# One ring of seven latent buffers instead of four and three, and five small cached loads issued by gpsimd instead of sync

## The chip, the cores and the metric

The kernel runs on 1 core of one Trainium2 chip. The metric is the device time of one execution in microseconds, shown as the median of the runs of the kernel before. The profile is of one further execution.

## The reference, cut to what matters

Two layers of a streaming encoder are computed for one prompt of 512 frames and one sample of 64 frames (576 columns in all; 128 further positions come from caches). Layer A is chunk-band attention; layer B, in which the change lies, is latent attention:

```python
def b_project(h, pos, w_in, g_qa, w_uq, g_kva, g_qn, g_qr, g_kr):
    cq, ckv, kr, g = jnp.split(h @ w_in, [B_Q_RANK, B_Q_RANK + B_KV_RANK, B_Q_RANK + B_KV_RANK + B_ROPE], axis=-1)
    q = (rmsnorm(cq, g_qa) @ w_uq).reshape(b, s, B_HEADS, B_QK)
    q_nope = rmsnorm(q[..., :B_NOPE], g_qn)
    q_rope = rope(rmsnorm(q[..., B_NOPE:], g_qr), pos)
    ckv = rmsnorm(ckv, g_kva)
    k_rope = rope(rmsnorm(kr, g_kr), pos)
    return q_nope, q_rope, ckv, k_rope, g

# sample: ckv and k_rope are put behind the cached latents
ckv_all = jnp.concatenate([ckv_cache.astype(ckv.dtype), ckv], axis=1)
kr_all = jnp.concatenate([kr_cache.astype(k_rope.dtype), k_rope], axis=1)
# every layer: y = x + (silu(g) * attention(...)) @ w_out
```

The ranks of cq and ckv are 512 each, there are 16 heads, the no-position part of a head has 128 elements and the rotary part 64.

## The kernel before, in words

All tensors are held transposed: 128 partitions of features by 576 columns of tokens. Every float32 product is made as three matmuls of a high and a low part (`mm3`, line 226, through `matmul`, line 164), so each operand is first split: ACT makes the high part (line 203, or 208 with a gain) and DVE the low part (lines 204, 209). A weight block of 128 x 512 is loaded by sync (`wload`, line 217) into one of three raw buffers and split into one of five pairs.

The work of TensorE is put in order by hand: the class `Order` (line 42) holds streams (Python generators) with ranks and a clock of its own, and the stream of the lowest rank that is due emits its next matmuls. The orders of the other engines and of the two DMA queues (sync and gpsimd) come from a scheduler that sees the tile pools. A tile of a pool with n buffers waits until the last reader of the buffer that it gets is done. Engines and queues run strictly in order: one waiting instruction holds all behind it.

Layer B begins at line 860, when layer A's sum lies in DRAM as x1d. Its 16 parts are loaded again on the gpsimd queue (line 885, tiles `bx`, one `raw` buffer each) and split into `bh` and `bl` with the gain of the norm. Three kinds of streams then run side by side:

- `latents` (line 976) multiplies 11 blocks of `wb_in` with all 16 parts (tiles `lat`, 96 matmuls each): 0 to 3 give cq, then 8 the rotary key, 4 to 7 ckv, and 9 and 10 the first two gates. In the stage of the queries it fills the time between their blocks.
- `queries` (line 985) follows when cq is normed: 24 blocks (tiles `u`, 24 matmuls each) in eight rounds of one rotary pair `r` and two heads `q`.
- every block has a chain. `raw_of` (line 490) is ACT's copy out of PSUM into a `raw` buffer, which gives the PSUM buffer back; there are two of them (tag `mm`), and an unfinished `lat` block holds one, so a `u` block needs the copy of the `u` before it. Then ACT squares and splits (lines 457, 203), DVE makes the low part (204), TensorE sums over the partitions (tiles `st`), ACT does Ln, Exp, Square (470, 478, 480) and DVE two steps and the scaling (481, 484, 488). `query_chain` (line 1002) writes the raw buffer to DRAM on the gpsimd queue (line 1007, tensor `qd`). `rotary_chain` (line 1011) swaps 32-row pieces by four DMAs of the sync queue (`sw`, line 916), combines them on DVE (917 to 919), splits the result (`hi` on ACT, `lo` on DVE) and writes four pieces on the sync queue (`qrd`, lines 1023, 1024). `rotary_key` (line 957) does the same with the key and writes `krT` on gpsimd (line 963).

The `raw` buffers lie in two pools, one of four and one of three (`lr0`, `lr1`, line 870). The 16 `bx` take turns by the list `turn`; cqraw and ckvraw name the four (`of=0`), krraw and every q and r the three (`of=1`). A ckvraw keeps its buffer until all four are scaled, after the last query.

The cached latents `cc` (four of 128 x 128, line 946) and the cached rotary key `krc` (line 966) share one buffer of their own and are loaded by the sync queue.

Of the kernel before, what the change touches and what calls it, by code (L numbers as in the profile page):

```python
# [15 lines left out]
F32 = mybir.dt.float32  # L16
# [4 lines left out]
P = 128  # L21
# [4 lines left out]
N = NS + NP  # L26
# [92 lines left out]
def encoder(tc, xT, wa_in, wa_out, wb_in, wuq, wuk, wuqr, wuv, wb_out, kcT, vc, ckvcT, krcT, gains, rtab,  # L119
            ident, cosT, sinT, yT, kT, vT, ckvT, krT):  # L120
    nc = tc.nc
# [4 lines left out]
    def pool(name, bufs=1, side="left", space=None):  # L126
        kw = dict(name=name, bufs=bufs)
        if space is None:
            kw["side"] = side
            kw["reuse_waits"] = "tile"  # L130
        else:
            kw["space"] = space
        g = tc.tile_pool(**kw)
        return g, g.__enter__()

    def close(g):
        g.__exit__(None, None, None)
# [17 lines left out]
    def two(ap):  # L155
        return ap.rearrange("p (c n) -> p c n", c=2)
# [44 lines left out]
    def split(src, hi, lo):  # L201

        ACT.copy(hi, src)  # L203
        V.tensor_tensor(out=lo, in0=src, in1=hi.bitcast(F32), op=ALU.subtract)  # L204
# [209 lines left out]
    def square_sum(acc, src, tp, w, first, name):  # L414

        if first:
            ACT.activation(acc, src, AF.Square)
            return
        sq = tp("s1", F32, name + "sq")[:, :w]
        ACT.activation(sq, src, AF.Square)  # L420
        V.tensor_tensor(out=acc, in0=acc, in1=sq, op=ALU.add)

    def col_sums(sq, tp, w, ones_ap, name, wait=2.0):

        s2 = tp("s2", F32R, name + "s2")[:, :w]
        s3 = tp("s3", F32R, name + "s3")[:, :w]
        split(sq, s2, s3)
        h = w // 2
        yield od_.now + wait
        yield "st"  # L430
        st = ps_of("st", name + "st")
        for j, s in enumerate((s2, s3)):
            for c in range(2):
                matmul(st[:, c, :h], ones_ap, s[:, c * h:(c + 1) * h], start=j == 0, stop=j == 1)
        return st, sq, s2
# [19 lines left out]
    def squares(src, tp, w, ones_ap, name):  # L455
        sq = tp("s1", F32, name + "sq")[:, :w]
        ACT.activation(sq, src, AF.Square)
        return (yield from col_sums(sq, tp, w, ones_ap, name, L_SQ))

    def rnorm(sums, n, w, base=None, coef=None, keep=None):  # L460

        st, t, y = sums
        h = w // 2
        plain = base is None and keep is None
        ms = st[:, :, :h]
        if plain:
            ACT.activation(two(t), ms, AF.Ln, scale=1.0 / n, bias=epst[:, 0:1])  # L470
        else:
            if base is None:
                V.tensor_scalar_add(two(keep), ms, n * EPS)
                ms = two(keep)
            else:
                V.scalar_tensor_tensor(out=ms, in0=two(base), scalar=coef, in1=ms, op0=ALU.mult, op1=ALU.add)
            ACT.activation(two(t), ms, AF.Ln, scale=1.0 / n)
        ACT.activation(y, t, AF.Exp, scale=-0.5)
        y = y.bitcast(F32)
        ACT.activation(t, y, AF.Square)  # L480
        V.scalar_tensor_tensor(out=two(t), in0=ms, scalar=n * EPS if plain else 0.0, in1=two(t),
                               op0=ALU.add, op1=ALU.mult)
        od_.give("st", L_ST)
        V.scalar_tensor_tensor(out=t, in0=t, scalar=3.0 * n, in1=y, op0=ALU.subtract, op1=ALU.mult)
        return t

    def scaled(raw, col, z):
        V.scalar_tensor_tensor(out=raw, in0=raw, scalar=col, in1=z, op0=ALU.mult, op1=ALU.mult)

    def raw_of(ps, tp, w, name, **kw):  # L490
        raw = tp("raw", F32, name, **kw)[:, :w]
        ACT.copy(two(raw), ps[:, :, :w // 2])  # L492
        od_.give("mm", L_M)
        return raw
# [372 lines left out]
    close(g_T)  # L867
    g_x1, x1p = pool("x1", side="right")
    g_l, lp = pool("lat")
    g_r0, lr0 = pool("latraw0")  # L870
    g_r1, lr1 = pool("latraw1")
    turn = [1, 1, 1, 0, 0, 0, 0]

    def tpl(tag, dt, name, of=None):
        if tag == "raw":
            turn.append(turn.pop(0))
            k = turn[-1] if of is None else of
            return (lr0, lr1)[k].tile([P, N], dt, tag=tag, bufs=(4, 3)[k], name=name)
        bufs = {"s1": SB, "s2": SB, "s3": S3}.get(tag, 1)
        return lp.tile([P, N], dt, tag=tag, bufs=bufs, name=name)  # L880

    h = []
    for m in range(KT):
        x1 = tpl("raw", F32, f"bx{m}")
        nc.gpsimd.dma_start(x1, x1d[m * P:(m + 1) * P, :])
        hi = x1p.tile([P, N], F32R, tag="x1", bufs=32, name=f"bh{m}")
        lo = x1p.tile([P, N], F32R, tag="x1", bufs=32, name=f"bl{m}")
        split_g(x1, gn[:, G_LNB + m:G_LNB + m + 1], hi, lo)
        h.append((hi, lo))
# [21 lines left out]
    def rope(x, name):  # L911

        sw = tpl("sw", F32, name + "sw")
        for j in range(4):
            i = j ^ 1
            nc.sync.dma_start(sw[j * 32:(j + 1) * 32, :], x[i * 32:(i + 1) * 32, :])
        V.tensor_tensor(out=x, in0=x, in1=cos, op=ALU.mult)
        V.tensor_tensor(out=sw, in0=sw, in1=sin, op=ALU.mult)
        V.tensor_tensor(out=x, in0=x, in1=sw, op=ALU.add)
# [2 lines left out]
    ckv_acc = lp.tile([P, N], F32, name="ckv_acc")  # L922

    def q_latent(m, ps):
        raw = raw_of(ps, tpl, N, f"cqraw{m}", of=0)
        raws.append(raw)
        square_sum(cq_acc, raw, tpl, N, m == 0, f"cq{m}")
        if m < 3:
            return
        mine = raws[:]  # L930
        raws.clear()
        yield lambda: flag["ln"]
        st = yield from col_sums(cq_acc, tpl, N, ones, "cq", 6.0)
        z = rnorm(st, 512, N, base=EX, coef=512 * EPS / D)
        for j in range(4):
            scaled(mine[j], gcq[:, j:j + 1], z)
            split(mine[j], *cq[j])
        yield od_.now + L_CQ
        flag["cq"] = True

    def kv_latent(m, ps):
        raw = raw_of(ps, tpl, N, f"ckvraw{m}", of=0)
        raws.append(raw)
        square_sum(ckv_acc, raw, tpl, N, m == 0, f"ckv{m}")
        cc = lp.tile([P, NC], F32, tag="cc", bufs=1, name=f"cc{m}")
        nc.sync.dma_start(cc, ckvcT[m * P:(m + 1) * P, :])
        split(cc, ckv[m][0][:, :NC], ckv[m][1][:, :NC])
        if m < 3:
            return
        st = yield from col_sums(ckv_acc, tpl, N, ones, "ckv", 6.0)  # L950
        z = rnorm(st, 512, N, base=EX, coef=512 * EPS / D)
        for j in range(4):
            scaled(raws[j], gkva[:, j:j + 1], z)
            nc.gpsimd.dma_start(ckvT[j * P:(j + 1) * P, :], raws[j])
            split(raws[j], ckv[j][0][:, NC:], ckv[j][1][:, NC:])

    def rotary_key(ps):

        raw = raw_of(ps, tpl, N, "krraw", of=1)
        st = yield from squares(raw, tpl, N, blk, "kr")  # L960
        scaled(raw, gkr, rnorm(st, 64, N, base=EX, coef=64 * EPS / D))
        rope(raw, "kr")
        nc.gpsimd.dma_start(krT, raw[:64, :])
        split(raw, KR[0][:, NC:], KR[1][:, NC:])
        cc = lp.tile([P, NC], F32, tag="cc", bufs=1, name="krc")
        nc.sync.dma_start(cc, krcT)
        split(cc, KR[0][:, :NC], KR[1][:, :NC])

    def gate_of(hd, ps, tp):
# [31 lines left out]

    def query_chain(hd, ps):
        n_ = f"q{hd}"
        raw = raw_of(ps, tpl, N, n_ + "raw", of=1)
        st = yield from squares(raw, tpl, N, ones, n_)
        scaled(raw, gqn, rnorm(st, P, N))
        nc.gpsimd.dma_start(qd[hd * P:(hd + 1) * P, :], raw)
        yield od_.now + L_CH
        flag["rot"] += 1

    def rotary_chain(pr, ps):
        n_ = f"r{pr}"
        raw = raw_of(ps, tpl, N, n_ + "raw", of=1)
        st = yield from squares(raw, tpl, N, blk, n_)
        scaled(raw, gqr, rnorm(st, 64, N))
        rope(raw, n_)
        hi = tpl("qrh", F32R, n_ + "hi")
        lo = tpl("qrl", F32R, n_ + "lo")
        split(raw, hi, lo)
        for j in range(2):  # L1020
            a = slice(j * 64, j * 64 + 64)
            r0 = (2 * pr + j) * P
            nc.sync.dma_start(qrd[r0:r0 + 64, :], hi[a, :].bitcast(F32))
            nc.sync.dma_start(qrd[r0 + 64:r0 + 128, :], lo[a, :].bitcast(F32))
        yield od_.now + L_CH
        flag["rot"] += 1
# [2 lines left out]
    od_.spawn(5, latents())  # L1029
    od_.spawn(3, queries())  # L1030
    od_.run()
    close(g_r1)
    close(g_r0)
    close(g_l)


# [226 lines left out]
DIRECT, GA, WRAW, WHL, SGB, DEEP, VA = 2, 2, 3, 5, 2, 2, 2  # L1263
LAT = (0, 1, 2, 3, 8, 4, 5, 6, 7, 9, 10)
LAHEAD = 1
SB, S1H, S2H, S3 = 4, 3, 1, 1
S1A, S2A, S3A, L_RS = 3, 2, 1, 5.0
L_SQ, L_RN, L_SP, L_X, L_SM, L_T, L_RE, L_CH, L_ST = 7.0, 11.5, 4.6, 2.3, 3.5, 2.9, 1.2, 4.0, 4.0

# [81 lines left out]
```

## Time and profile before

| what | value |
|---|---|
| three runs | 2080.25, 2077.2, 2077.83 us; median 2077.83 us |
| profiled execution | 2074.61 us, its span 2072.8 us, granted clock 0.987 |
| PE (TensorE) | 2002.1 us busy (97%), 14692 matmuls |
| DVE (VectorE) | 1353.6 us busy (65%), 2651 instructions |
| ACT (ScalarE) | 1107.8 us busy (53%), 2034 instructions |
| POOL (GpSimd) | 91.8 us busy (4%), 173 instructions |
| sync queue | 171.78 MB, 30.6% of the 16 DMA engines' time |
| gpsimd queue | 49.20 MB, 6.8% |

The span runs from the first to the last instruction; 1.8 us of the execution lie around it. Layer A takes the time up to about 1137 us, the latents and queries of layer B that from 1146 to 1426 us, the heads of layer B and its output the rest. A matmul of 288 columns follows the one before it every 0.13 us at the upper of the two clock levels (2.4 GHz) and every 0.27 us at the lower (1.2 GHz), so a busy PE can still lose time.

### The profile page before, as it was taken

How to read it: one execution, taken by the hardware profiler on the slowest of the kernel's cores; microseconds unless marked ns; L12 is line 12 of the kernel's file. 1: busy time of each engine (PE TensorE's matmuls, PEld its weight loads, DVE VectorE, ACT ScalarE, POOL GpSimd, SP SyncE). 2: the span in 40 equal slices, each digit the busy share in tenths (PEclk: the TensorE clock that was granted, in tenths of full speed). 3: DMA queues.
4: the chain of work that ended last, by engine and by line, in shares of the span. 5: the costliest groups of instructions: out<-in, count | busy, mean ns of one | idle time of the engine just before them, and what ended most of it. 6: DMA issues, size and time to landing. Idle time of an engine off the chain costs nothing. (4 is left out here: it accounts for less than half of the span.)

```text
span 2072.8 us, 37566 instructions
## 1 busy us (share of the span) xinstructions
PE 2002.1 (97%) x14692; PEld 1979.3 (95%) x14692; DVE 1353.6 (65%) x2651; ACT 1107.8 (53%) x2034; POOL 91.8 (4%) x173
## 2 busy tenths in 40 slices
PE   8999999999999999999999898889999999999998
PEld 8999999999999999999999898889999999998998
DVE  7665555555555555559777456667776767676875
ACT  6644454454544444456444457666666656664432
POOL 0000000000000000000001000000000000002000
PEclk9999999999999999999999999999999999999999
DMA  7333333333333333324553434444232332256541
GB/s 209 86 83 88 93 84 89 93 78 88 89 88 88 90 87 86 87 73 139 156 155 112 147 84 127 127 112 145 76 91 81 90 90 80 74 154 217 173 139 61
DMA packets 119345, 223.38 MB, mean 108 GB/s; under 512 B 14272, under 2 KB 29264, under 8 KB 119168
## 3 DMA queue, kind: packets, MB, share of 16 engines
q1 hardware_dynamic: 104752, 171.78, 30.6%
q0 software_dynamic: 14416, 49.20, 6.8%
q8 instruction: 115, 1.88, 0.4%
q14 instruction: 62, 0.51, 0.1%
HBM read 183.92 MB, written 34.36 MB: 105 GB/s over the span
## 5 line engine op out<-in xcount | busy, mean ns | idle before, releaser
L204 DVE TENSOR_TENSOR wa_2l<-wa_2r,wa_2h 128x512 fp32r<-128x512 f32 x61 | 42.2, 692 | 92.2 <-ACT wa_2h L203 92.2
L203 ACT CAST wa_2h<-wa_2r 128x512 fp32r<-128x512 f32 x61 | 37.7, 619 | 103.7 <-PE a2p L164 10.1
L204 DVE TENSOR_TENSOR wa_3l<-wa_3r,wa_3h 128x512 fp32r<-128x512 f32 x61 | 42.2, 692 | 43.8 <-ACT wa_3h L203 42.3
L203 ACT CAST wa_0h<-wa_0r 128x512 fp32r<-128x512 f32 x61 | 37.8, 619 | 61.3 <-PE a2p L164 4.3
L203 ACT CAST wa_3h<-wa_3r 128x512 fp32r<-128x512 f32 x61 | 37.7, 618 | 51.2 <-PE a2p L164 4.5
L164 PE MATMUL u<-cqh,wq_0h 128*128 128x288 f32 x128 | 31.7, 333 | 24.6 <-ACT r4raw L492 5.2
L204 DVE TENSOR_TENSOR wa_0l<-wa_0r,wa_0h 128x512 fp32r<-128x512 f32 x61 | 41.9, 687 | 18.0 <-ACT wa_0h L203 18.0
L203 ACT CAST wa_1h<-wa_1r 128x512 fp32r<-128x512 f32 x61 | 37.8, 620 | 25.0 <-PE a0pg L164 2.6
L204 DVE TENSOR_TENSOR wa_1l<-wa_1r,wa_1h 128x512 fp32r<-128x512 f32 x61 | 41.9, 686 | 11.7 <-ACT wa_1h L203 11.7
L164 PEld LDWEIGHTS u<-cqh,wq_0h 128*128 128x128 f32 x128 | 23.6, 217 | 26.4 <-ACT r4raw L492 5.4
L164 PE MATMUL u<-cql,wq_0h 128*128 128x288 f32 x128 | 30.5, 324 | 0.0
L164 PE MATMUL u<-cqh,wq_0l 128*128 128x288 f32 x128 | 30.3, 322 | 0.0
L204 DVE TENSOR_TENSOR wb_1l<-wb_1r,wb_1h 128x512 fp32r<-128x512 f32 x25 | 17.2, 688 | 19.9 <-ACT wb_1h L203 19.8
L204 DVE TENSOR_TENSOR wb_3l<-wb_3r,wb_3h 128x512 fp32r<-128x512 f32 x25 | 17.2, 687 | 17.6 <-ACT wb_3h L203 17.5
L164 PE MATMUL lat<-bh,wb_0h 128*128 128x288 f32 x88 | 19.5, 304 | 9.1 <-ACT bh L208 9.1
L203 ACT CAST wb_1h<-wb_1r 128x512 fp32r<-128x512 f32 x25 | 15.5, 619 | 23.4 <-PE lat L164 10.0
L203 ACT CAST wb_3h<-wb_3r 128x512 fp32r<-128x512 f32 x25 | 15.4, 617 | 23.3 <-PE lat L164 11.2
L204 DVE TENSOR_TENSOR wb_2l<-wb_2r,wb_2h 128x512 fp32r<-128x512 f32 x25 | 17.1, 686 | 13.0 <-ACT wb_2h L203 13.0
L164 PE MATMUL g<-bh,wb_1h 128*128 128x288 f32 x112 | 24.3, 298 | 0.0
L164 PE MATMUL g<-bh,wb_0h 128*128 128x288 f32 x112 | 24.3, 298 | 0.0
L164 PE MATMUL g<-bh,wb_2h 128*128 128x288 f32 x112 | 24.2, 298 | 0.0
L164 PE MATMUL g<-bh,wb_3h 128*128 128x288 f32 x112 | 24.2, 298 | 0.0
(6782 smaller groups left out, 8058.5 us busy)
## 6 DMA issues: line engine op xcount, KB each, us to landing
wa_0r<-wa_in SPq DMA_DIRECT2D x61, 256.0 KB, 2.9
wa_1r<-wa_in SPq DMA_DIRECT2D x61, 256.0 KB, 2.9
wa_2r<-wa_in SPq DMA_DIRECT2D x61, 256.0 KB, 2.9
wa_3r<-wa_in SPq DMA_DIRECT2D x61, 256.0 KB, 2.9
wb_0r<-wb_in SPq DMA_DIRECT2D x25, 256.0 KB, 3.0
wb_1r<-wb_in SPq DMA_DIRECT2D x25, 256.0 KB, 3.0
wb_2r<-wb_in SPq DMA_DIRECT2D x25, 256.0 KB, 2.9
wb_3r<-wb_in SPq DMA_DIRECT2D x25, 256.0 KB, 2.9
```

What stands on the lines that cost most here:

```text
L164: nc.tensor.matmul(out, lhs, rhs, start=start, stop=stop, **kw)
L203: ACT.copy(hi, src)
L204: V.tensor_tensor(out=lo, in0=src, in1=hi.bitcast(F32), op=ALU.subtract)
```

## The change

The two pools become one pool of seven buffers, and the list `turn` and the argument `of` go: each `raw` tile gets whichever of the seven the scheduler gives it. The five small loads `cc` and `krc` move from the sync queue to the gpsimd queue.

```diff
-    g_r0, lr0 = pool("latraw0")
-    g_r1, lr1 = pool("latraw1")
-    turn = [1, 1, 1, 0, 0, 0, 0]
-
-    def tpl(tag, dt, name, of=None):
+    g_r, lrp = pool("latraw")
+
+    def tpl(tag, dt, name):
         if tag == "raw":
-            turn.append(turn.pop(0))
-            k = turn[-1] if of is None else of
-            return (lr0, lr1)[k].tile([P, N], dt, tag=tag, bufs=(4, 3)[k], name=name)
+            return lrp.tile([P, N], dt, tag=tag, bufs=RAWB, name=name)
...
-        nc.sync.dma_start(cc, ckvcT[m * P:(m + 1) * P, :])
+        nc.gpsimd.dma_start(cc, ckvcT[m * P:(m + 1) * P, :])
...
-        raw = raw_of(ps, tpl, N, n_ + "raw", of=1)
+        raw = raw_of(ps, tpl, N, n_ + "raw")
...
-        nc.sync.dma_start(cc, krcT)
+        nc.gpsimd.dma_start(cc, krcT)
...
-SB, S1H, S2H, S3 = 4, 3, 1, 1
+RAWB, SB, S1H, S2H, S3 = 7, 4, 3, 1, 1
```

The order of TensorE's instructions is the same in both programs. On the other engines the scheduler gives another order. Three places follow.

The first is ACT in the stage of the queries, where the second rotary pair is copied out of PSUM (`r2raw<-u`); q3's and q2's rows are the norms of heads 3 and 2, `wb`, `wr` and `wq` are weight blocks.

```order
 L203 CAST wb_3h<-wb_3r 128x512
+L492 COPY r2raw<-u_14640 128x576
+L457 ACTIVATE r2sq<-r2raw 128x576
+L203 CAST r2s_14675<-r2sq 128x576
 L203 CAST wr_0h<-wr_0r 128x512
 L470 ACTIVATE q3sq<-q3st,epst 128x576
+L478 ACTIVATE q3s_14606<-q3sq 128x576
+L480 ACTIVATE q3sq<-q3s_14606 128x576
 L203 CAST r1hi<-r1raw 128x576
-L492 COPY r2raw<-u_14643 128x576
-L457 ACTIVATE r2sq<-r2raw 128x576
-L203 CAST r2s_14678<-r2sq 128x576
```

The copy and the two rows behind it stand ahead of the norm of q3 and of r1's split now, where they stood behind them; the copies of r3 to r7 move in the same way. In the program before, r2raw waits for the write of q2 to DRAM, two blocks back; in the changed one for that of q0, five blocks back.

The second is ACT at the start of layer B, before and (the second fence) in the change: `KRh` is the high part of the cached rotary key, `ckvh` that of a cached latent, and `lnb_s` the last row that belongs to layer A's sum.

```order
L203 CAST lnb_s_13309<-lnb_acc 128x576
L203 CAST KRh<-krc 128x128
L208 ACTIVATE bh_13329<-bx_13327,gn 128x576
L208 ACTIVATE bh_13335<-bx_13333,gn 128x576
L208 ACTIVATE bh_13341<-bx_13339,gn 128x576
L203 CAST ckvh_13299<-cc_14467 128x128
```

```order
L203 CAST lnb_s_13309<-lnb_acc 128x576
L208 ACTIVATE bh_13326<-bx_13324,gn 128x576
L208 ACTIVATE bh_13332<-bx_13330,gn 128x576
L203 CAST KRh<-krc 128x128
L208 ACTIVATE bh_13338<-bx_13336,gn 128x576
L208 ACTIVATE bh_13344<-bx_13342,gn 128x576
```

The first two `bh` stand ahead of `KRh` now, and the four `ckvh` have gone behind the last `bh`.

The third is the gpsimd queue at the same place in the changed program.

```order
L834 DMA x1d<-x_15_13046 128x576
L891 DMA sin<-sinT 128x576
L962 DMA krc<-krcT 128x128
L881 DMA bx_13366<-x1d 128x576
...
L881 DMA bx_13414<-x1d 128x576
L942 DMA cc_14464<-ckvcT 128x128
```

`krc` is new between `sin` and the eighth `bx`, and the four `cc` follow the last `bx`; the next row of that queue, `krT`, comes some 80 us later in the profile of before.

## Rows read from the trace of the kernel before

**Rows 1.** Busy time by stretch: PE, PEld, DVE, ACT, POOL, then PEclk, DMA share, GB/s.

```profile
1233.00:1410.40 177.40, 147.07 (x1013) 144.71 (x1012) 120.67 (x172) 123.53 (x196) 8.72 (x16) 0.91 0.46 124
1165.00:1228.00 63.00, 63.00 (x475) 63.00 (x475) 25.43 (x37) 24.59 (x42) 0.00 (x0) 1.00 0.32 81
...
1390.00:1400.00 10.00, 10.00 (x77) 10.00 (x77) 5.75 (x8) 8.44 (x14) 0.00 (x0) 1.00 0.30 73
```

**Rows 2.** Waits of PE over the span: us in total, times, longest us.

```profile
PE lat L164 <- ACT bh L208: 9.1, 1, 9.1
...
PE u L164 <- ACT q1raw L492: 5.6, 1, 5.6
...
PE u L164 <- ACT r6raw L492: 4.8, 1, 4.8
...
PE u L164 <- ACT r5raw L492: 3.4, 1, 3.4
...
PE u L164 <- ACT q6raw L492: 0.2, 1, 0.2
```

**Rows 3.** Chain of waits, 1312 to 1339 us: start, us, what.

```profile
1312.08 4.06 DMA qd<-q6raw
...
1316.91 5.07 PE u L164 x24
1321.98 2.40 PE lat L164 x18
1324.38 0.54 PE r4st L164 x4
1324.92 3.19 PE u L164 x24
1328.11 1.60 PE lat L164 x12
```

**Rows 4.** Timeline of ACT around two of the waits: start, us, instruction, [idle before].

```profile
1309.38 0.62 ACT L203 CAST wq_0h<-wq_0r 128x512 fp32r<-128x512 f32 x1 [0.74 <-PE u L164]
...
1316.22 0.64 ACT L492 COPY r4raw<-u 128x576 f32<-128x576 f32 x1 [2.27 <-DMA qd<-q6raw]
...
1368.95 0.63 ACT L492 COPY q12raw<-u 128x576 f32<-128x576 f32 x1
...
1385.20 0.64 ACT L492 COPY r7raw<-u 128x576 f32<-128x576 f32 x1 [0.20 <-DMA qd<-q12raw]
```

**Rows 5.** Timeline of ACT and DVE: the rotary pair 3, from its copy to its split.

```profile
1294.42 0.64 ACT L492 COPY r3raw<-u 128x576 f32<-128x576 f32 x1
...
1318.99 0.75 DVE L204 TENSOR_TENSOR r3lo<-r3raw,r3hi 128x576 fp32r<-128x576 f32 x1
```

**Rows 6.** Timeline of SP's queue and of ACT: a weight load behind the rotary writes.

```profile
1312.18 0.33 SPq L217 DMA_DIRECT2D wb_0r<-wb_in  x1
1318.88 1.12 SPq L1023 DMA_DIRECT2D qrd<-r3hi  x2
...
1323.13 0.33 SPq L217 DMA_DIRECT2D wq_0r<-wuq  x1
...
1333.19 0.62 ACT L203 CAST wq_0h<-wq_0r 128x512 fp32r<-128x512 f32 x1 [0.66 <-PE u L164]
```

**Rows 7.** Timeline of ACT and POOL at the start of layer B.

```profile
1138.82 0.54 POOL L895 DMA_DIRECT2D sin<-sinT  x1
...
1145.53 0.30 ACT L203 CAST KRh<-krc 128x128 fp32r<-128x128 f32 x1 [5.28 <-DMA krc<-krcT]
1145.74 2.10 ACT L208 ACTIVATE bh<-bx,gn 128x576 fp32r<-128x576 f32 x3
...
1161.51 0.78 ACT L208 ACTIVATE bh<-bx,gn 128x576 fp32r<-128x576 f32 x1
```

**Rows 8.** DMA issues, 1120 to 1175 us: count, KB each, median us to landing.

```profile
bx<-x1d POOLq DMA_DIRECT2D x16, 288.0 KB, 4.5
...
sin<-sinT POOLq DMA_DIRECT2D x1, 288.0 KB, 7.3
...
krc<-krcT SPq DMA_DIRECT2D x1, 64.0 KB, 7.9
```

More of the change, by code (lines that the diff above doesn't have):

```diff
@@ L488, in scaled, with raw_of @@
         V.scalar_tensor_tensor(out=raw, in0=raw, scalar=col, in1=z, op0=ALU.mult, op1=ALU.mult)
-    def raw_of(ps, tp, w, name, **kw):
-        raw = tp("raw", F32, name, **kw)[:, :w]
+    def raw_of(ps, tp, w, name):
+        raw = tp("raw", F32, name)[:, :w]
         ACT.copy(two(raw), ps[:, :, :w // 2])
@@ L924, in q_latent @@
     def q_latent(m, ps):
-        raw = raw_of(ps, tpl, N, f"cqraw{m}", of=0)
+        raw = raw_of(ps, tpl, N, f"cqraw{m}")
         raws.append(raw)
@@ L941, in kv_latent @@
     def kv_latent(m, ps):
-        raw = raw_of(ps, tpl, N, f"ckvraw{m}", of=0)
+        raw = raw_of(ps, tpl, N, f"ckvraw{m}")
         raws.append(raw)
@@ L957, in rotary_key @@
     def rotary_key(ps):
-        raw = raw_of(ps, tpl, N, "krraw", of=1)
+        raw = raw_of(ps, tpl, N, "krraw")
         st = yield from squares(raw, tpl, N, blk, "kr")
@@ L1012, in rotary_chain @@
         n_ = f"r{pr}"
-        raw = raw_of(ps, tpl, N, n_ + "raw", of=1)
+        raw = raw_of(ps, tpl, N, n_ + "raw")
         st = yield from squares(raw, tpl, N, blk, n_)
@@ L1031, in encoder @@
     od_.run()
-    close(g_r1)
-    close(g_r0)
+    close(g_r)
     close(g_l)
```

## The prediction, made before the changed kernel was run

> **What bounds the kernel now.** I read the busy times by stretch first, then TensorE's waits, the chain of waits, and the timelines. TensorE (PE) is the bound, so time can only come from stretches where it idles or runs at its lower clock. In the undisturbed stretch 1165 to 1228 us it does 475 matmuls in 63.00 us, 0.1326 us each. In the stage of the queries, 1233 to 1410.4 us, it does 1013 [rows 1]. At that pace they take 1013 x 0.1326 = 134.4 us; the stage lasts 177.4. So 43.0 us are lost here: 177.4 - 147.07 = 30.3 idle, and 147.07 - 134.4 = 12.7 in matmuls at the lower clock (the granted clock of the stage is 0.91).
>
> The idle time is seven waits of 3.4 to 5.6 us, six of them at the copy of a rotary pair and one at q1's (the first, the third and the last are in [rows 2]). The chain shows what each is: the write of q6 to DRAM is issued at 1312.08 and takes 4.06 us; only then can ACT copy r4 out of PSUM, into the buffer that q6 leaves, and only then can PE begin the next u block, which needs that PSUM buffer [rows 3, 4]. At q1 it is the write of the rotary key, at r6 the split of r5, both in the same role. With three buffers for 24 blocks each rotary copy gets the buffer of a q two blocks back. The copy of q12 comes at 1368.95 and its write releases r7 at 1385.20 [rows 4]: a q holds a buffer for 16.2 us, longer than two blocks last. Behind most waits the next 24 matmuls run slow: 5.07 us for the u block behind r4's, 3.19 for one at the full clock [rows 3].
>
> **The ring, stage of the queries.** In the changed order each of these copies takes the buffer of a block four or five steps back (krraw, r or q), not two or three. A round of three u blocks takes, without waits, 3 x 3.19 + 2.40 + 1.60 + 2.40 + 3 x 0.54 = 17.6 us [rows 3], 5.9 a block. Four blocks are 23.5 us against 16.2 for a q. The closest call for a q is q14, which gets q12's buffer three blocks on: 17.6 against 16.2. A rotary pair holds its buffer for 25.3 us (r3, from 1294.42 to 1318.99 + 0.75 [rows 5]); the closest call is q12, which gets r5's after four blocks, 23.5 us. That may cost about 2 us once, and the copy has some 2 us of room before PE needs it (12 lat matmuls, 1.60, and a sum, 0.54 [rows 3]). So the seven waits go, and the slow matmuls with them: 43.0 us at most.
>
> What is late next? ACT is busy 123.53 us in this stage and DVE 120.67 [rows 1]; of 134.4 us that is 92% and 90%. Both must still come in time, in order, without the rest that the waits gave them. The price of this shows in no row, so I bound it. From below: between the waits PE already runs some 17 us on end, and the waits in there are three of 0.2 us (one is in [rows 2]), 0.6 in all. From above: in the ten us from 1390, when PE never paused, ACT was busy 8.44 [rows 1]; if it can't do more than 84%, the stage lasts 123.53 / 0.844 = 146.4 us, 12.0 more than 134.4, and slow matmuls at the old ratio (12.7 for 30.3) add 5.0: 17.0 in all. I take 6, nearer to the lower end because ACT still idles for PE right ahead of such a wait (0.74 us at 1309.38 [rows 4]), so it is ahead there. **Gain of the stage: 43.0 - 6 = 37 us**, between 26.0 and 42.4.
>
> **The small loads, start of layer B.** PE waits 9.1 us for the first `bh` [rows 2]. ACT stands idle 5.28 us until the cached key has landed at 1145.5, 7.9 us after its issue, then runs its split and the 16 `bh`, the last at 1161.51 + 0.78 = 1162.29 [rows 7, 8]. In the changed order two `bh`, whose parts came early, go ahead of the wait, and the four `ckvh` leave this stretch. The key is now issued behind `sin`, at about 1138.82 + 0.54 = 1139.4, in the same queue. If it lands just behind `sin`, at 1138.82 + 7.3 = 1146.1 [rows 7, 8], ACT has from there its split (0.30), 14 `bh` of 0.70 (2.10 for three [rows 7]), three weight splits of 0.62 [rows 4] and three steps of the norm, which I put at the same 0.7: 0.3 + 9.8 + 1.9 + 2.1 = 14.1 us, ending at 1160.2, 2.1 us sooner. Bounds: if it took 9.9 us it would land at 1149.3 and all the gain and 1.1 more be lost; I set the lower end at -1. If it landed as soon as a median `bx` (4.5 us [rows 8]), at 1143.9, 4.3 are won; with the later `bx` issued sooner I set the upper end at 5. **I take 2.** Off sync's queue five issues go; it has room, since no PE wait names a load. On gpsimd's queue four `cc` now wait for one buffer; the next row there, `krT`, comes 80 us later, so they hold up nobody.
>
> The Trainium skill, "DMA: Bandwidth & Descriptors", section "Queues, rings and completion order", says that each DMA engine takes turns between the queue rows that have work; a small load alone in sync's row would get its turn soon, and one behind five large transfers in gpsimd's row must wait for them. By that rule the move itself costs time; the row of the key on sync (7.9 us for 64 KB, longer than any 288 KB `bx` median) does not show such an early turn [rows 8]. By the rule the term would be about 0 instead of 2, and the time 2041 instead of 2039.
>
> **Sum.** 37 + 2 = 39 us. The profiled execution took 2074.61 us, which would become 2035.6; the median of the three runs stands 3.2 above it, so on the scale of the runs 2077.83 - 39 = **2039 us**. The bounds of this case: 42.4 + 5 gives 2030.4, 26.0 - 1 gives 2052.8. After the stage I count nothing: 120 lat matmuls (16 us) stand between the last sum and the first block of the heads and cover the ckv chain as before; if that chain came more than that late, it would cost its excess.
>
> **The rivals.**
>
> *ACT or DVE sets the pace, chance 0.14.* For it: 92% and 90% in engines that wait in order for each other. Against it: in the rows ACT waits for PE, not PE for ACT, outside the ring's waits. Price: the upper bound above, 17.0 us lost: gain 26.0 + 2, **2050 us**.
>
> *The waits come back late in the stage, chance 0.06.* Each ckvraw keeps a buffer of the same ring to the end, so it shrinks from seven to three, where before they had buffers of their own. If r6 and r7 wait as now, 4.8 and 3.7 us (r6's is in [rows 2]), with 12.7 / 30.3 of slow matmuls on top, 12.0 of the gain go: 27, **2051 us**. Against it: the late distances of three and four blocks worked out above.
>
> *The change does not do what it says, chance 0.05.* If the waits are not the buffers' but the chains' own pace (ACT's copies stand in order behind norms, and q9's norm came right before r5's copy), only the start is won: 2 us, **2076 us**.
>
> *Slower, chance 0.05: the sync queue starves PE of weights.* It runs in order; after the load of 1312.18 it is held until r3's split at 1318.88 and issues the next weight load at 1323.13; ACT splits that at 1333.19 [rows 6]. Now the ring's waits hold PE back by 43.0 / 8 = 5.4 us a round; without them PE runs ahead of the rotary chain, whose swaps and splits hold this queue. Of the 10.1 us from issue to split a landing takes some 4.5 [rows 8], and the issue stood free for another 1.8 us before 1323.13, the writes ending at about 1321.3 (four of 0.6 from 1318.88). So the hold may come 7.4 us later at no cost; each us more costs a us a round. From 12.8 us later per round on, the kernel is slower than before; at 14 it is 8 x 1.2 - 2 = 8 us slower, **2086 us**. Against it: the hold is some 9 us now and tied to chains that get no longer.
>
> **How the numbers follow.** The main case has 0.70, the rivals 0.14, 0.06, 0.05 and 0.05. The range runs from the best bound of the main case, 2031, to 2054, just past its worst bound and both rivals that keep part of the gain; with the tails of the main case cut it holds some 0.85. Within 0.2% (4.2 us, about what a measurement of this kernel can tell from no change) lies only the third rival: 0.05. Faster by more: 0.90. Slower: 0.05.
>
> **What would show it.** Right: in the waits of PE the seven u rows of 3 us and more are gone, the stage between the same matmuls lasts 135 to 150 us with a granted clock near 1.00, ACT is busy about 90% of it, and the last `bh` ends some 39 - 37 = 2 us sooner after the end of layer A. The first rival shows as many waits of 0.5 to 2 us on `st` or u blocks for ACT or DVE; the second as waits at r6, r7 or a ckvraw; the fourth as PE or ACT waiting for a wq, wr or wb load. I am wrong if the stage stays above 155 us, or if the gain lies elsewhere.

## The result, and the profile after

The change takes 2028.93 us (median of 4 runs, 2025.97 to 2030.18) against 2078.0 us (2077.2 to 2080.25) for the kernel before: a ratio of 0.976, 95% interval 0.9743 to 0.9777, 49 us less. The forecast was 2039, its range 2031 to 2054: the sign and the place were right, the size was 10 us too small.

The profiled execution of the change took 2030.18 us, its span 2028.4 us. The busy times of its engines:

```profile
PE 1989.9 (98%) x14692; PEld 1968.7 (97%) x14692; DVE 1349.2 (67%) x2651; ACT 1104.8 (54%) x2034; POOL 94.0 (5%) x178
```

Waits of PE in the stage of the queries, where [rows 2] had seven of 3.4 to 5.6 us:

```profile
PE u L164 <- ACT q6raw L492: 0.5, 1, 0.5
PE u L164 <- ACT q11raw L492: 0.2, 1, 0.2
PE u L164 <- ACT r1raw L492: 0.2, 1, 0.2
```

The three small ones were there before and are all that is left. The same stage, between the same 1013 matmuls as in [rows 1], by stretch (us, busy PE, PEld, DVE, ACT, POOL, clock, DMA share, GB/s):

```profile
1229.70:1366.25 136.55, 135.66 (x1013) 134.72 (x1012) 117.85 (x172) 121.17 (x196) 8.69 (x16) 1.00 0.59 161
```

177.40 us became 136.55, the clock went from 0.91 to 1.00, ACT is busy 89% of the time. At full pace 1013 matmuls take 134.4 us, so 2.2 us are left: 0.9 idle and 1.3 in matmuls somewhat late. The chain of waits shows the place of r4's copy, as [rows 3] did, now without the write of q6 ahead of the u block and at the upper clock:

```profile
1292.27 3.20 PE u L164 x24
1295.46 2.40 PE lat L164 x18
1297.86 0.54 PE r4st L164 x4
1298.40 2.65 PE u L164 x20
```

At the start of layer B, ACT now makes two `bh`, waits for the key, and goes on (timeline of ACT; it answers to [rows 7]):

```profile
1138.10 1.44 ACT L208 ACTIVATE bh<-bx,gn 128x576 fp32r<-128x576 f32 x2
1144.88 0.30 ACT L203 CAST KRh<-krc 128x128 fp32r<-128x128 f32 x1 [5.34 <-DMA krc<-krcT]
1145.08 3.43 ACT L208 ACTIVATE bh<-bx,gn 128x576 fp32r<-128x576 f32 x5
```

The wait is as long as before (5.28 us), it only stands two parts later. The five parts split in one go behind it were there already. PE's wait for the first `bh`, 9.1 us before, is down to 6.9 in two pieces:

```profile
PE lat L164 <- ACT bh L208: 6.9, 2, 3.5
```

To see where the 44.4 us between the two profiled executions lie (2074.61 - 2030.18), I set the start of the same matmuls side by side:

```
                                       before   change   sooner by
ao14a in layer A, 13 before its last   1135.5   1133.4     2.1
sum of the rotary key (krst)           1224.1   1220.8     3.3
sum of q0 (q0st)                       1238.8   1235.5     3.3
first block of the heads (b0k)         1426.2   1382.0    44.2
end of the span                        2072.8   2028.4    44.4
```

The stage of the queries gave 40.9 us, the start of layer B 1.2. Another 2.1 came in layer A, which the change doesn't touch, and 0.2 behind the stage. Between the medians lie 4.6 us more (49.07 against 44.43).

### The profile page after: what moved, and what is told of

It reads as the page before. It is cut to its first block, busy times and chain, and to the rows that moved or that the text cites. A ratio compares the mean times of both kernels' runs of the same rounds, so it can differ in the third digit from the quotient of the medians.

```text
span 2028.4 us, 37554 instructions
## 1 busy us (share of the span) xinstructions
PE 1989.9 (98%) x14692; PEld 1968.7 (97%) x14692; DVE 1349.2 (67%) x2651; ACT 1104.8 (54%) x2034; POOL 94.0 (5%) x178
## 4 chain that ended last, share of the span: by engine, by line
PE 86%; issue 8%; DVE 2%; DMA 2%; ACT 1%; POOL 1%; SPq 0%; POOLq 0%; DVEq 0%; ACTq 0%
PE g L164 8%; PE lat L164 6%; PE u L164 3%; PE a2p L164 3%; PE ao L164 3%; PE a5p L164 3%; PE a14p L164 3%; PE a9p L164 3%; PE a7p L164 3%; PE a8p L164 3%; PE a13p L164 3%; PE a12p L164 3%; PE a10p L164 3%; PE a11p L164 3%; PE a4p L164 3%
## 5 line engine op out<-in xcount | busy, mean ns | idle before, releaser
L203 ACT CAST wa_2h<-wa_2r 128x512 fp32r<-128x512 f32 x61 | 37.7, 619 | 103.7 <-PE a2p L164 10.1
L203 ACT CAST wb_1h<-wb_1r 128x512 fp32r<-128x512 f32 x25 | 15.5, 619 | 16.5 <-PE lat L164 7.7
L164 PE MATMUL g<-bh,wb_0l 128*128 128x288 f32 x112 | 24.0, 296 | 0.0
L164 PE MATMUL g<-bh,wb_1l 128*128 128x288 f32 x112 | 24.0, 296 | 0.0
```

The source lines that it names most:

```text
L164: nc.tensor.matmul(out, lhs, rhs, start=start, stop=stop, **kw)
```

## The experiments

**The ring alone, and the loads alone.** Two kernels with one part of the change each.

```diff
# ring of seven, loads on sync        # two pools of before, loads on gpsimd
-nc.gpsimd.dma_start(cc, ...)         -nc.sync.dma_start(cc, ...)
+nc.sync.dma_start(cc, ...)           +nc.gpsimd.dma_start(cc, ...)
```

> The change with the five small loads left on the sync queue (the ring of seven alone). Theory: nearly all of the gain is the stage of the queries, which between the first q0 sum and the first b0k fell from 187.4 to 146.5 us in the two profiles; that stays, so 2030 us, 0.5 to 2 us slower than the change because the start of layer B (layer A's end to the key's sum) goes back from its new length to that of before, 1.2 us longer. The waits of TensorE in the stage are the three of 0.2 to 0.5 us. Rival: sync's queue is what starved the stage, and moving its five loads away gave a good part; then the waits at rotary copies come back and the time is above 2040 us.

Measured: 2030.83 us (2030.32 to 2031.44), ratio 0.9769 (0.9756 to 0.9782), as expected.

> The kernel before with the five small loads on the gpsimd queue (two pools of four and three kept). Theory: only the start of layer B moves, by the 1.2 us that the two profiles show there, so 2077 us (2074 to 2079), and the seven waits of 3.4 to 5.6 us at copies into the ring of three are all there. Rival: the loads are worth several us because they free sync's queue in the stage; then 2070 us or less, with fewer or shorter waits.

Measured: 2076.21 us (2071.78 to 2080.6, 12 runs) against 2078.96 (2072.56 to 2082.47, 17 runs), ratio 0.9988 (0.9977 to 0.9999). Its waits of PE, the first and the last of the seven:

```profile
PE u L164 <- ACT q1raw L492: 5.6, 1, 5.6
...
PE u L164 <- ACT r5raw L492: 3.4, 1, 3.4
```

What follows: each part does its own share. The ring carries the stage (146.2 us from the q0 sum to b0k, in the change 146.5, before 187.4); with it alone, sync's queue still holds the five loads and starves nobody. The loads carry the start: from the ao14a matmul of the table above to the sum of the key pass 88.6, 89.6 and 88.9 us in three profiles with the key on sync, and 87.4, 86.5, 86.5 and 86.4 in four with it on gpsimd, 2.3 us less in the mean (three more profiles of kernels below, with 86.8 to 87.5, make it 2.2). This share is small beside the 9 to 10 us over which the runs of these two kernels spread, so it is told by the profiles and not by the times.

**A ring of six.** `RAWB = 6` instead of 7.

> The change with six buffers. ACT now has the copies of r6 and r7 behind the splits of r5 and r6 again, where the kernel before had them. Theory: from there on one buffer is missing, so two to three waits of 3 to 5 us with slow matmuls behind them return, late in the stage: 8 to 15 us more than the change, 2037 to 2044 us; the waits at q1 and at r2 to r5 stay away. Rival: the distance of the buffers did not matter and only the order of ACT did: then within 2 us of the change.

Measured: 2047.4 us (2043.82 to 2049.7), 18 us more than the change, above the 8 to 15 expected. Waits of PE in the stage and behind it:

```profile
PE u L164 <- ACT r6raw L492: 4.8, 1, 4.8
PE u L164 <- ACT r7raw L492: 3.7, 1, 3.7
...
PE ckvst L164 <- ACT ckvs L203: 2.2, 1, 2.2
...
PE ckvst L164 <- DVE ckvs L204: 0.7, 1, 0.7
```

The waits come back where the ckvraw have taken three of the six buffers, with the lengths of before to 0.1 us, at r6 and r7 alone. What I had left out is the third: the copy of the last ckvraw now waits for the write of q14, and the sum of ckv waits 2.9 us. Timeline of ACT:

```profile
1380.60 0.64 ACT L492 COPY ckvraw<-lat 128x576 f32<-128x576 f32 x1 [1.00 <-DMA qd<-q14raw]
```

From the q0 sum to b0k PE idles 12.4 us here and 0.9 in the change, and its matmuls take 7.6 us more; together these are the 19.1 us by which the stage (165.6 us) is longer. So it is the count of buffers that decides, and six are too few; more than seven were not run. With six the scheduler also put the copies of r6 and r7 behind the splits again, so this run does not part the buffers from the order that follows from them. That it is the buffer which ACT waits for is read from what ended its waits: the write of q6 in [rows 4], the write of q14 here.

**The kernel before, profiled again.** No edit.

> The kernel before, profiled a second time, to see what of its time changes from execution to execution. Its first profiled execution took 2074.61 us against 2078.0 of the unprofiled runs. Theory: the seven waits have the same lengths within 0.3 us, and what differs is for how many matmuls the granted clock is low behind them (12.7 us in the first profile) and behind the 1.9 us wait at about 1010 us in layer A, where the first profile shows a clock of 0.91 and the change 1.00. If the profile lands at 2077 to 2080 us, the extra 3 to 5 us should be slow matmuls at these places. Rival: the waits themselves differ by us, from DMA landings.

Measured: 2078.39 us in its profiled execution, 3.8 more than the first. By stretch: the first row is the one block looked at below, the second the stage, beside [rows 1]:

```profile
1296.88:1303.60 6.72, 6.72 (x30) 6.49 (x30) 2.58 (x5) 2.37 (x4) 0.54 (x1) 0.59 0.51 132
1233.70:1416.05 182.35, 151.99 (x1013) 149.54 (x1012) 120.72 (x172) 123.57 (x196) 8.69 (x16) 0.89 0.46 121
```

Idle are 182.35 - 151.99 = 30.4 us, as before (30.3); the matmuls took 17.6 us longer than at full pace, where the first profile had 12.7 and the kernel with the loads alone 16.2. The stage is 5.0 us longer than in the first profile and the start of layer B 1.0; the part behind the stage is 1.9 shorter. Behind r3's wait the difference is plain. Timeline of PE, kernel before, first profile, and then the same 30 matmuls by stretch:

```profile
1295.11 0.53 PE L164 MATMUL u<-cqh,wq_0h 128*128 128x288 f32 x2 [3.56 <-ACT r3raw L492]
...
1299.48 0.53 PE L164 MATMUL u<-cqh,wq_0h 128*128 128x288 f32 x2 [0.21 <-ACT q6raw L492]
```

```profile
1295.11:1299.27 4.16, 4.16 (x30) 3.94 (x30) 2.60 (x5) 2.35 (x4) 0.54 (x1) 1.00 0.82 213
```

and the timeline in the second profile:

```profile
1296.88 0.85 PE L164 MATMUL u<-cqh,wq_0h 128*128 128x288 f32 x2 [3.62 <-ACT r3raw L492]
...
1299.92 0.68 PE L164 MATMUL u<-cqh,wq_0h 128*128 128x288 f32 x2
1300.40 0.68 PE L164 MATMUL u<-cql,wq_0h 128*128 128x288 f32 x2
...
1303.77 0.53 PE L164 MATMUL u<-cqh,wq_0h 128*128 128x288 f32 x2 [0.17 <-ACT q6raw L492]
```

The wait is the same to 0.06 us; behind it the clock granted was 1.00 in one execution and 0.59 in the other, 2.56 us apart for 30 matmuls. In the slow rows two matmuls start every 0.48 us, so one every 0.24 us, and not every 0.27 as the text ahead of the prediction has it. So the theory holds in the stage: the waits stay the same to 0.2 us, what they cost behind them does not.

**The change again, and more work on ACT.** One kernel is the change itself, as the measure; the other two put copies that nobody reads into each q chain.

```diff
-        scaled(raw, gqn, rnorm(st, P, N))
+        z = rnorm(st, P, N)
+        scaled(raw, gqn, z)
+        ACT.copy(z, raw)        # twice for 32
```

> The change once more, as the measure for the kernels beside it and for what varies. Theory: the random part of the time of the kernel before came from the slow matmuls behind its eight long waits; with seven of these gone the runs lie closer together than the 10 us of before (2072.56 to 2082.47): within 5 us, around 2029 us, and the stage of the queries has 0.5 to 1.5 us of waits and under 2 us of slow matmuls in this profile too. Rival: the spread is general, and stays at 8 us or more.

Measured: 2029.8 us (2027.76 to 2031.71, 4 us), ratio 0.9784 (0.9769 to 0.9798) to 2075.29. The stage is 146.4 us long, and PE idles 0.7 us in it. Over both sets its 8 runs span 5.7 us; those of before span 9.9 over 17 runs, 6.1 over 7 and 4.0 over 9, so a narrower spread of the change is not shown.

> The change with 16 more copies of 128x576 on ACT in the stage of the queries, one in each q chain behind the scaling, beside the path (nobody reads the copy); results are unchanged. ACT's busy time in the stage goes from 121.2 to about 131.4 us of 136.5, 96%. Theory: ACT and DVE cost nothing as long as their sum fits beside TensorE, so 0 to 3 us more than the change. Rival, the term of the prediction that put a price on their lateness: ACT can keep up only to a share near that reached in the change (89%); then the stage lasts 131.4 / 0.89 = 148 us or more, 11 us more than the change.

Measured: 2032.14 us (2029.38 to 2033.32), 2.3 above the change run again; stage 149.8. By stretch:

```profile
1229.00:1368.40 139.40, 135.71 (x1008) 134.01 (x1006) 117.49 (x172) 128.07 (x211) 8.68 (x16) 1.00 0.58 157
```

> As the one with 16, with two such copies in each q chain: 32 more, ACT busy about 141.7 us, more than the 136.5 that the stage lasts in the change. Theory: now ACT sets the pace, at nearly full load: the stage lasts 142 to 150 us, 6 to 14 us more than the change, some of it slow matmuls behind new waits at copies out of PSUM. Rival (a share near 0.89 at most): 141.7 / 0.89 = 159 us, 23 us more.

Measured: 2033.78 us (2032.34 to 2035.38), 4.0 above, where 6 to 14 were expected; stage 151.9. By stretch:

```profile
1227.90:1369.90 142.00, 137.24 (x1014) 134.97 (x1014) 119.16 (x173) 133.72 (x226) 8.68 (x16) 1.00 0.57 154
```

A copy added some 0.4 us to ACT's busy time where I had put 0.64 (it lasts 0.66, but ACT's instructions overlap), so ACT came to 92% and 94% and not to 96% and above 100%. Still they tell the two views apart. There is no ceiling near 89%: ACT does 94%. Nor is its work free up to 100%: 6.9 us more cost 3.4 of stage, 12.5 more cost 5.5, about 0.45 us a us, in small waits of PE and some slow matmuls. Two of the waits with 16:

```profile
PE r1st L164 <- DVE q1sq L481: 1.6, 1, 1.6
...
PE ckvst L164 <- DVE q15sq L481: 0.9, 1, 0.9
```

PE waits there for DVE to free the one PSUM buffer of the sums. At the first of them DVE itself had waited 1.3 us for ACT just before:

```profile
1246.05 0.76 DVE L204 TENSOR_TENSOR r0lo<-r0raw,r0hi 128x576 fp32r<-128x576 f32 x1 [1.34 <-ACT r0hi L203]
```

**The same on DVE.** `V.tensor_copy(z, raw)` in place of the copy on ACT, 16 times.

> The change with 16 more copies of 128x576 on DVE instead of ACT, one in each q chain behind the scaling; results are unchanged. The 16 on ACT took the stage from 136.5 to 139.4 us at 128.1 us of ACT, 32 took it to 142.0 at 133.7: about 0.4 us a us. DVE is at 118 us here and goes to about 125 to 129. Theory: DVE has the more room, so the stage gets 0 to 3 us longer. Rival: DVE's chain decides as much as ACT's (TensorE's new waits with ACT's copies were at DVE steps), and it costs the same 3 us or more.

Measured: 2028.48 us (2028.2 to 2030.01), as the change within the spread of its runs; the stage 147.6, 1.1 longer. By stretch:

```profile
1228.00:1365.00 137.00, 135.30 (x1009) 134.17 (x1008) 122.36 (x186) 121.34 (x196) 9.35 (x16) 1.00 0.58 160
```

4.5 us more on DVE cost 1.1 us, so it has the more room. A copy also holds the two buffers that it reads and writes for longer, on either engine. That most of the 3.4 us with ACT are ACT's own work is likely by this pair, but not shown.

**The start of layer B, three ways.** The first loads the key ahead of cos and sin, and the latents during the queries.

```diff
+    cc = lp.tile([P, NC], F32, tag="cc", bufs=1, name="krc")
+    nc.gpsimd.dma_start(cc, krcT)
+    split(cc, KR[0][:, :NC], KR[1][:, :NC])
     h = []
...
-        cc = lp.tile([P, NC], F32, tag="cc", bufs=1, name=f"cc{m}")
+        cc = tpl("sw", F32, f"cc{m}")[:, :NC]
```

> The change with the cached rotary key loaded ahead of cos and sin on the gpsimd queue (its load and split written ahead of the reloads of layer A's sum), and the four cached latents loaded during the queries, in turns with the swapped pieces in their buffer. In the change ACT stands idle 5.34 us for the key, up to 1144.88, with reloaded parts already there (five parts are split in one go behind it, and the reloads behind them wait 5.71 us for their buffers). Theory: with the key there at about 1139 the parts follow at once, the first latent block ends 3 to 5 us sooner: 2024 to 2026 us beside the change's 2029. Rival: the reloads themselves land no sooner than that (issued at 1133.60, median 5.2 us, in a queue with 64 KB to 288 KB loads before them), so ACT waits for parts instead and the gain is under 1 us; or the four late loads hold the swaps back and add 1 to 3 us to the stage.

Measured: 2029.49 us (2027.71 to 2030.48), no gain. Timeline of ACT:

```profile
1142.24 0.30 ACT L203 CAST KRh<-krc 128x128 fp32r<-128x128 f32 x1 [3.10 <-DMA krc<-krcT]
1142.44 4.77 ACT L208 ACTIVATE bh<-bx,gn 128x576 fp32r<-128x576 f32 x7
```

The key came sooner, but its split now stood ahead of all parts, and seven of them waited for it: the edit left the wait in place. The key's sum comes 85.6 us after the ao14a matmul, 1.1 sooner than in the four profiles above, and the later loads cost 0.7 in the stage (147.2). The second version gives the key a buffer of the ring, which is free only behind the last reload:

```diff
-        cc = lp.tile([P, NC], F32, tag="cc", bufs=1, name="krc")
+        cc = tpl("raw", F32, "krc")[:, :NC]
...
-        cc = lp.tile([P, NC], F32, tag="cc", bufs=1, name=f"cc{m}")
+        cc = tpl("sw", F32, f"cc{m}")[:, :NC]
```

> The change with the cached rotary key loaded into a buffer of the ring behind the last reload of layer A's sum, its split on ACT now some 80 us later, and the four cached latents loaded in turns with the swapped pieces. In the run before this one (key early) the first split of ACT still waited 3.10 us for the key, which took 6.6 us to land behind two reloads of 288 KB, with seven parts ready behind it. Theory: it is the wait of ACT for the small load, in whatever queue, that costs; without it the first seven parts are split from 1138 us on, buffers come free 3 to 6 us sooner, and the key's sum comes 2 to 4 us sooner after layer A's end than in the change (87.4 and 86.5 us in its two profiles): 2025 to 2028 us beside 2029. Rival: the reloads behind the seven land late all the same, and nothing is won beyond 1 us.

Measured: 2026.07 us (2024.89 to 2026.85), ratio 0.9759 (0.9746 to 0.9773). Timeline of ACT:

```profile
1137.42 4.77 ACT L208 ACTIVATE bh<-bx,gn 128x576 fp32r<-128x576 f32 x7
1143.76 0.78 ACT L208 ACTIVATE bh<-bx,gn 128x576 fp32r<-128x576 f32 x1 [1.57 <-DMA bx<-x1d]
```

The wait for the key is gone, PE waits 3.5 us for the first `bh` where it had waited 6.9 in the change, and the key's sum comes 82.5 us after the ao14a matmul, 4.2 sooner than in the four profiles above; the later loads cost 0.7 in the stage (147.2). That makes 3.5 us, as expected, and the run stands 3.7 below the change run again. The two were measured at different times, and beside the kernel before of its own time the change had 0.976 and 0.9784, this one 0.9759: the gain is told by the profiles and not by the intervals.

The third keeps this and loads cos and sin on the sync queue:

```diff
-    nc.gpsimd.dma_start(cos, cosT)
-    nc.gpsimd.dma_start(sin, sinT)
+    nc.sync.dma_start(cos, cosT)
+    nc.sync.dma_start(sin, sinT)
```

> As the run beside it, with cos and sin (288 KB each, used 80 us later) loaded by the sync queue as well, so that the gpsimd queue holds only the reloads of layer A's sum here. ACT's order is the same. Theory: a transfer on the same queue lies ahead of the reloads in time; two such loads of 288 KB out of the way let the eighth part and those behind it land 1 to 2 us sooner: 1 to 2 us faster than the run beside it. Rival: sync's weight loads for the first latent block are now behind cos and sin, and TensorE waits for a weight split instead: 1 to 4 us slower.

Measured: 2024.99 us (2024.28 to 2026.06), beside 2026.07. Timeline of ACT:

```profile
1139.94 4.77 ACT L208 ACTIVATE bh<-bx,gn 128x576 fp32r<-128x576 f32 x7
1146.34 0.78 ACT L208 ACTIVATE bh<-bx,gn 128x576 fp32r<-128x576 f32 x1 [1.63 <-DMA bx<-x1d]
```

Neither view is borne out: the eighth part comes no sooner (1.63 us of waiting against 1.57), the stretch lasts the same 82.5 us, no weight is late. The runs of the two overlap, so the 1 us between them is not settled. Both beat the kernel before; their medians stand 3 to 5 us below those of the change.

## Why the prediction was right or wrong

**What held.** The mechanism: seven waits for the write or split of a block two or three back, gone with buffers four and five back, and the slow matmuls with them. The closest calls that I named came as worked out: q14 waits for nothing, q12 has ACT wait 0.3 us for r5's split and PE not at all. Of the rivals, the late ring waits did not come (they do with six buffers), the change did what it says, and sync's queue starved nobody: in the waits of ACT over the stage, all that names a weight load is

```profile
ACT wq_0h L203 <- DMA wq_0r<-wuq: 1.2, 2, 0.7
```

The term for the start, 2 us, was right in size: 1.2 in the first pair, 2.3 in the mean of the profiles. So was its working: the key was issued at 1137.28 and landed 0.4 us behind `sin`, and the gain came from the order of ACT, two `bh` ahead of the wait and the `ckvh` out of the way. The rule of the Trainium skill that I set against it ("DMA: Bandwidth & Descriptors", "Queues, rings and completion order") would have had the term at about 0. No run here tests that rule, and my reading of [rows 8] against it was wrong: I took the key to be alone in sync's row, and it was not. In the kernel before, two weight blocks were issued there just ahead of it (DMA issues of 1135 to 1138 us):

```profile
wb_0r<-wb_in SPq DMA_DIRECT2D x1, 256.0 KB, 5.1
wb_1r<-wb_in SPq DMA_DIRECT2D x1, 256.0 KB, 6.7
krc<-krcT SPq DMA_DIRECT2D x1, 64.0 KB, 7.9
```

The 64 KB took 7.5 to 7.9 us in this place on sync's row (three profiles), 5.9 to 7.6 behind the large loads on gpsimd's (seven), and 2.0 to 2.1 where all loads before it had landed (the second and third version of the start). How soon a small load alone in its row gets its turn stays open.

**What failed, first: "I take 6" for the pace of ACT and DVE.** It was 2.2 (136.55 - 134.4). Its upper end came from a stretch of ten us in which ACT was busy 84% with PE never pausing; I read that as what ACT can do, and it was only what it was given to do. With more work it does 94%. That is 3.8 us of the miss; the start's 0.8 short in the first pair goes against it.

**Second: "the median of the three runs stands 3.2 above it, so on the scale of the runs 2077.83 - 39".** This carries the distance between the profiled execution and the median over to the new kernel as a constant. The change's profile stands 1.25 above its median, not 3.2 below: 4.5 us of the miss. A part of these was loss that the change could take away. The 12.7 us of slow matmuls behind the waits are one draw: 17.6 and 16.2 in two other profiles with the same waits. The granted clock of whole executions points the same way: of the 17 runs of the kernel before, the six at 0.984 took 2078.2 to 2082.5 us, the five at 0.985 took 2075.7 to 2081.1, the five at 0.986 or 0.987 took 2075.8 to 2077.6, and the one at 0.989 took 2072.56. The profiled execution that I went by had 0.987, so it had drawn low. With 15.5, the mean of the three, in place of 12.7, the stage's loss is 30.3 + 15.5 = 45.8, and the forecast would have been near 2036 with the 6, near 2032 with the 2.2. The range went wrong the same way: its best end, 42.4 + 5, took 12.7 as fixed. The other 1.7 of the 4.5 us no run places: the profile of the loads alone lost 16.2 us there and was yet the fastest of its twelve runs.

**Third, by chance:** 2.1 us in layer A, told below, and 0.2 behind the stage; no step of mine could claim them. Together: 3.8 - 0.8 + 2.3 + 4.5 = 9.8 of the 10.1; the rest is rounding.

## What to carry to other kernels

Count for every buffer of a ring how long its last reader holds it and how many blocks later it is asked for; if one write to DRAM or one split stands between, a pooled ring can buy with no memory at all what a split one loses; here one buffer less brought two of the seven waits back at full length, and a new one. When TensorE's waits go, the matmuls behind them speed up as well, and that part is to be taken from several executions, since a single profile shows one draw. A small load whose split stands in an in-order engine's list ahead of ready work holds that work until it lands, on either of the two queues here: place its split, not only its issue.

## What the runs showed of the hardware that I had not expected

The same wait of TensorE is followed by a different clock from one execution to the next: 1.00 or 0.59 behind r3's 3.6 us, as shown above. And a wait that differs by a few tenths of a us can be followed by either level. In layer A, at ao4a's wait for DVE, PE stood 0.5 to 2.1 us, by execution. Kernel before, waits and stretch:

```profile
PE ao4a L164 <- DVE x L405: 1.9, 1, 1.9
```

```profile
1000.00:1020.00 20.00, 18.10 (x126) 17.90 (x125) 15.17 (x25) 7.02 (x12) 0.54 (x1) 0.91 0.41 126
```

and the change:

```profile
PE ao4a L164 <- DVE x L405: 1.6, 1, 1.6
```

```profile
1000.00:1020.00 20.00, 18.45 (x140) 18.25 (x139) 15.57 (x26) 7.75 (x13) 0.54 (x1) 1.00 0.44 138
```

In the four profiles with 1.9 to 2.1 us here (the kernel before twice, the ring of six, cos and sin on sync) the clock of this stretch is 0.91, in the other nine, with 0.5 to 1.6, it is 1.00. With 0.3 us more of wait, 14 matmuls fewer fell into the 20 us, 1.9 us of work. That is nearly all of the 2.1 us of layer A, in a place that no kernel here changes; why DVE is later there in some executions stays open.
